# Ninety-six elementwise operations of a decoder layer's weight preparation put on GpSimd

## The chip, the cores and the metric

The kernel runs on one core of one Trainium2 chip. The metric is the device time of one execution in microseconds (us). The engines are TensorE (PE, with its weight loads as PEld), VectorE (DVE), ScalarE (ACT), GpSimd (POOL) and SyncE (SP), which issues nearly all DMA transfers.

## The reference

One decoder layer over 2048 tokens of width 1024, in float32:

```
h = rms_norm(x, mix_norm_g);  z = h @ w_in
y_lru = rg_lru(causal_dwconv(lru_x, 4 taps)) * gelu(lru_gate)
c     = silu(layer_norm(causal_dwconv(conf_a * sigmoid(conf_b), 31 taps)))
x = x + concat(y_lru, c) @ w_out

h = rms_norm(x, xa_norm_g);  m = rms_norm(mem, mem_norm_g)      # mem: 256 tokens
q = h @ w_q;  k, v = split(m @ w_kv)                            # 4 heads of 256
x = x + softmax(q k^T / 16) v @ w_o

h = rms_norm(x, ffn_norm_g);  g, u = split(h @ w_up)            # 2 x 3072
x = x + (gelu(causal_dwconv(g, 3 taps)) * u) @ w_down
return rms_norm(x, final_norm_g)
```

## The kernel before, in words

**Products.** Every large product is made of three matmuls on rounded operands: a value is split into a high part in TensorE's rounded format and a low part, the rest, and high by high, high by low and low by high are summed (`mm3`). `split(src, hi, lo)` does it: ScalarE copies the source into `hi`, VectorE subtracts `hi` from the source into `lo`. Tiles are 128 x 512.

**Tokens.** They are worked in four quarters of 512. A quarter's mixer computes the 31-tap convolution as 30 steps of VectorE on each of four blocks (`conf`), and the recurrence (`lru`). Quarters 0 and 1 then run `attend` alone. Quarters 2 and 3 run together in `attend_pair`, whose three products (with w_out, with the matrix A, with the matrix VO) are each done by seven block products in place of eight (`Folded`). Behind these come the up and down projections, more than half of the time, which use a like scheme.

**The matrices A and VO.** `memory_a` folds the query weights into the memory's keys, `memory_vo` the output weights w_o into its values. In `memory_vo`, for each of four heads, two pieces of w_o (128 x 1024, the tile `raw`) are loaded, each is split in two halves (tiles `wh`, `wl`), and TensorE multiplies the value rows (`kvh`, `kvl`) with them; the result is split again (`voh`, `vol`) and stored.

**The combined weights.** The seven products need sums and differences of blocks of the weights. `Folds.prepare` makes them once for each of the three matrices, as `F_out`, `F_a` and `F_vo`: for each of four block rows it gets four blocks by `block` (for w_out a load from memory, for A and VO the sum of the stored high and low parts, tile `wd`) and forms four sums or differences with `combine` (tiles `t`), which the SP queue stores as `t_out`, `t_a` and `t_vo`. `weight` fetches them back when the product comes and splits them. In each row T1 is the difference of two blocks, T3 and T2 need one block more (T2 needs T1 too), and T4 needs a fourth block and T2.

**The order of the work.** The kernel does not run its operations in the order of the program text. Tasks (generators) are stepped by a clock of TensorE's work; their operations are collected by `Program` and then planned: a list scheduler with a price for each operation and a due time worked back from TensorE's order gives each engine its fixed queue, and it also hands out the 84 buffers of 128 x 512. The order of the program text, and so the order in which buffers are handed out, depends on TensorE's clock alone. The prices for n columns are, in us, 0.15 + 0.0009 n for VectorE (0.2 for three-operand operations) and

```
    if eng == "Pool":
        return 0.18 + n * 0.0021
```

for GpSimd. No operation of the plan before is priced by this, since GpSimd gets none but some DMA issues at the start. All operations of the plan are emitted by one line, so the profile shows them as L399; they are told apart by their tiles.

Of the kernel before, what the change touches and what calls it, by code (L numbers as in the profile page):

```python
# [14 lines left out]
ALU = mybir.AluOpType  # L15
AX = mybir.AxisListType

P = 128
# [4 lines left out]
TT = 512  # L23
# [3 lines left out]
KH = D // P // 2  # L27
# [395 lines left out]
def hybrid_layer(  # L423
# [17 lines left out]
    pr = Program(nc, place)  # L441
# [4 lines left out]
    def V(name, *a, **k):  # L446
        pr.do("DVE", name, *a, **k)

    def ACT(out, in_, func, **k):
        pr.do("ACT", "activation", out, in_, func, **k)  # L450
# [14 lines left out]
    def ps():  # L465
        return pr.new("ps", name="ps")

    def tmp(name="tmp"):
        return pr.new("S", name=name)
# [4 lines left out]
    def pair(name, shape=None):  # L474
        return rnd(name + "h", shape), rnd(name + "l", shape)
# [99 lines left out]
        V("scalar_tensor_tensor", nsp[:], p[:], -2.0 * RG_C, neg[:], op0=ALU.mult, op1=ALU.add)  # L575


    def split(src, hi, lo):
        ACT(hi[:], src, AF.Copy)
        V("tensor_tensor", lo[:], src, hi[:].f32(), op=ALU.subtract)  # L580

    def split_scaled(src, g, hi, lo):
        ACT(hi, src, AF.Copy, scale=g)
# [2 lines left out]
    def mm3(p, wh, wl, xh, xl, start, stop, **k):  # L586
        matmul(p, wh, xh, start=start, stop=False, **k)
        matmul(p, wh, xl, start=False, stop=False, **k)
        matmul(p, wl, xh, start=False, stop=stop, **k)
# [44 lines left out]
    def raw_rows(w, r0):  # L634
        st = pr.new("W", (P, D), name="raw")
        pr.dma(st[:], w[r0 : r0 + P, :])
        return st

    def split_cols(st, f):
        hi, lo = pair("w", (P, KQ, P))  # L640
        split(st[:, :, f * P : (f + 1) * P], hi, lo)
        return hi, lo

    def flat(b):
# [2 lines left out]
    class Columns:  # L647
# [22 lines left out]
        def rounded(self, c0, kq, st):  # L670
            return [split_cols(st, f) for f in range(2)]
# [255 lines left out]
    def kv(c0):  # L927

        hi, lo = pair("kv")
        pp = [ps(), ps()]  # L930
        for kq in range(2):
            st = raw_cols(w_kv[0], c0, kq)
            for f in range(2):
                with together():
                    for k in range(KQ):
                        sl = slice((k % 2) * M, (k % 2 + 1) * M)
                        matmul(pp[f][:, :M], st[:, k, f * P : (f + 1) * P], mt[kq * 2 + k // 2][:, sl], start=kq + k == 0, stop=kq == 1 and k == KQ - 1)
            yield 0
        for f in range(2):
            fs = slice(f * M, (f + 1) * M)  # L940
            ACT(hi[:, fs], pp[f][:, :M], AF.Copy)
            V("tensor_tensor", lo[:, fs], pp[f][:, :M], hi[:, fs].f32(), op=ALU.subtract)
        return hi, lo

    def keep(rows, k, half, cols, src):

        base = (k * 2 + half) * 2
        for i in range(2):
            tok = rows.kept.tok.setdefault(base + i, Buf(None, (1,)))
            pr.dma(rows.kept.at(base + i)[:, cols], src[i].f32(), writes=[tok], join=True)  # L950
# [73 lines left out]
    def memory_vo():  # L1024
        yield mem_a
        yield VO_LATE
        for h in range(4):
            vh, vl = yield from kv(D + h * M)
            yield 1
            pp = [ps() for _ in range(4)]  # L1030
            for db in range(2):
                st = raw_rows(w_o[0], h * M + db * P)
                ww = []
                for half in range(2):
                    hi, lo = pair("w")
                    split(st[:, half * TT : (half + 1) * TT], hi, lo)
                    ww.append((hi, lo))
                for i, p in enumerate(pp):
                    mb, (wh, wl) = i // 2, ww[i % 2]
                    vs = slice(db * M + mb * P, db * M + (mb + 1) * P)  # L1040
                    with together():
                        mm3(p[:], vh[:, vs], vl[:, vs], wh[:], wl[:], db == 0, db == 1)
                    if i % 2:
                        yield 0
            for i, p in enumerate(pp):
                t = pair("vo")
                split(p[:], *t)
                keep(VO_rows, h * 2 + i // 2, i % 2, slice(0, TT), [b[:] for b in t])
# [276 lines left out]

    def combine(name, a, b, op):
        t = tmp(name)
        V("tensor_tensor", t[:], a, b, op=op)  # L1330
        return t

    UP_ORDER = ("B11", "B21", "T2", "T1", "T3", "T4", "B22")
# [237 lines left out]
    class Down:  # L1571
# [6 lines left out]
        def block(self, at, i):  # L1578
            m, f = at // NQ, at % NQ * KD + i
            t = tmp("h")  # L1580
            pr.dma(t[:], h_kept[f * P : (f + 1) * P, m * TT : (m + 1) * TT], reads=[h_tok[m // 2, f]])
            return t
# [71 lines left out]
    class Folds:  # L1654
# [5 lines left out]
        def block(self, k, half):  # L1660
            if self.rows.w is not None:
                t = tmp("wd")
                pr.dma(t[:], self.rows.w[k * P : (k + 1) * P, half * TT : (half + 1) * TT])
                return t
            hi, lo = self.rows.get(k, half)
            t = tmp("wd")
            V("tensor_tensor", t[:], hi[:].f32(), lo[:].f32(), op=ALU.add)
            return t

        def prepare(self, wait):  # L1670
            for i in range(KH):
                b11, b12 = self.block(i, 0), self.block(i, 1)
                t1 = combine("t", b12[:], b11[:], ALU.subtract)
                self.t.put(KH + i, t1[:])
                yield wait
                b22 = self.block(KH + i, 1)
                t3 = combine("t", b22[:], b12[:], ALU.subtract)
                t2 = combine("t", b22[:], t1[:], ALU.subtract)
                self.t.put(2 * KH + i, t3[:])
                self.t.put(i, t2[:])  # L1680
                yield wait
                t4 = combine("t", self.block(KH + i, 0)[:], t2[:], ALU.subtract)
                self.t.put(3 * KH + i, t4[:])
                del b11, b12, b22, t1, t2, t3, t4
                yield wait
            self.done.done = True
# [331 lines left out]
    m, n, a = mixers, normeds, attends  # L2018
# [6 lines left out]
    a[2].gen = attend_pair([n[2], attended[1]], [m[2], m[3], n[3]])  # L2025
    fold = Task(fold_weights())
    later.gen, mem_a.gen, mem_vo.gen = setup_later(), memory_a(), memory_vo()
    first_t.gen, first.gen, tail.gen = X[0].kept(a[1], T_PACE), first_x(), feed_forward()
    tasks.extend(TURNS())
# [33 lines left out]
```

## Time and profile before

| | us |
|---|---|
| median of 3 runs | 2397.0 (2396.76 to 2398.66) |
| span of the profiled execution | 2396.1 |
| granted TensorE clock, mean | 0.999 |
| busy: PEld | 1974.5 (82%) |
| busy: ACT | 1313.2 (55%) |

The profiled execution has no time of its own beside its span, which is 0.9 us under the median of the runs. A row of the profile names line, engine, operation and tiles (out<-in), the shapes, how often, and then busy time in us and the mean of one in ns; in a timeline it is start and length in us. A wait row names who waited, for whom, the total in us, how often and the longest. A matmul of 512 columns is recorded with 0.39 us, though the next one starts 0.23 us later: they overlap, and so do neighbouring VectorE operations, by less.

### The profile page before, as it was taken

To read this page: it belongs to the slowest core of one execution; us is meant where nothing else is said; L and a number is where in the kernel's file an instruction comes from. 1 tells how busy PE (TensorE), PEld (TensorE's weight loads), DVE (VectorE), ACT (ScalarE), POOL (GpSimd) and SP (SyncE) were. 2 spreads that over 40 slices of the span, in tenths; PEclk is the share of its full clock that TensorE was granted. 3 is DMA by queue.
4 is the path that set the end of the run, shared out by engine and by line. 5 is a ranking of instruction groups with operands and counts; after the bars stand their busy time and mean duration, and the time that the engine had idled before them with its cause. 6 is when DMAs were issued, how large, how long until landed. Compare 5 with 4: busy or idle time off the path is not lost.

```text
span 2396.1 us, 33483 instructions
## 1 busy us (share of the span) xinstructions
PE 2382.6 (99%) x10948; PEld 1974.5 (82%) x10948; DVE 2034.0 (85%) x3355; ACT 1313.2 (55%) x2374; POOL 11.2 (0%) x26
## 2 busy tenths in 40 slices
PE   9999999999999999999999999999999999999998
PEld 7898888888887888888888888888888888888887
DVE  7999994299899869879999887988988896676787
ACT  7772776357557678695555555554555541222333
POOL 1000000000000000000000000000000000000000
PEclk9999999999999999999999999999999999999999
DMA  9598789775878988787766544556565589887986
GB/s 351 197 296 309 234 300 305 254 255 176 296 261 271 318 277 280 268 289 265 252 234 208 194 172 158 175 177 211 190 216 199 186 303 324 283 280 254 312 303 258
DMA packets 363912, 604.56 MB, mean 252 GB/s; under 512 B 34809, under 2 KB 116985, under 8 KB 363738
## 3 DMA queue, kind: packets, MB, share of 16 engines
q1 hardware_dynamic: 362952, 601.81, 73.8%
q8 instruction: 86, 1.41, 0.2%
q14 instruction: 88, 0.72, 0.1%
q0 software_dynamic: 640, 0.36, 0.0%
q10 hardware_dynamic: 146, 0.27, 0.0%
HBM read 409.36 MB, written 192.94 MB: 251 GB/s over the span
## 4 chain that ended last, share of the span: by engine, by line
PE 94%; DVE 2%; ACT 2%; DMA 1%; issue 1%; SPq 0%; POOL 0%; DVEq 0%; POOLq 0%; ACTq 0%
PE ps L399 94%; DMA wl<-w_down 1%; DVE conv L399 1%; ACT L399 0%; DMA raw<-in_w_kv_dram 0%; ACT wh L399 0%; DVE wl L399 0%; ACT gate L399 0%; DVE x L399 0%; DVE s L399 0%; ACT yh L399 0%; DVE smalls L399 0%; DVE ptl L399 0%; ACT prob L399 0%; ACT conv L399 0%
## 5 line engine op out<-in xcount | busy, mean ns | idle before, releaser
L399 PE MATMUL ps<-Xh,wh 128*128 128x512 f32 x1344 | 523.3, 389 | 0.7 <-ACT u L399 0.7
L399 PE MATMUL ps<-Xh,wl 128*128 128x512 f32 x1344 | 523.2, 389 | 0.7 <-DVE wl L399 0.5
L399 PE MATMUL ps<-Xl,wh 128*128 128x512 f32 x1344 | 523.0, 389 | 0.0
L399 PE MATMUL ps<-wh,hidh 128*128 128x512 f32 x960 | 374.4, 390 | 0.0
L399 PE MATMUL ps<-wh,hidl 128*128 128x512 f32 x960 | 374.2, 390 | 0.1
L399 PE MATMUL ps<-wl,hidh 128*128 128x512 f32 x960 | 373.7, 389 | 0.0
L399 DVE SCALAR_TENSOR_TENSOR conv<-cb,v,conv 128x512 f32<-128x512 f32 x480 | 334.9, 741 | 1.8 <-ACT conv L399 0.9
L399 PEld LDWEIGHTS ps<-Xh,wl 128*128 128x128 f32 x1344 | 252.3, 188 | 54.0 <-DVE wl L399 1.5
L399 PEld LDWEIGHTS ps<-Xh,wh 128*128 128x128 f32 x1344 | 252.3, 188 | 53.1 <-ACT u L399 1.1
L399 PEld LDWEIGHTS ps<-Xl,wh 128*128 128x128 f32 x1344 | 252.3, 188 | 52.5
L399 ACT ACTIVATE hidh<-s 128x512 fp32r<-128x512 f32 x186 | 113.8, 631 | 271.6 <-DVE s L399 227.9
L399 PEld LDWEIGHTS ps<-wh,hidl 128*128 128x128 f32 x960 | 180.2, 188 | 39.5 <-DVE hidl L399 2.1
L399 PEld LDWEIGHTS ps<-wh,hidh 128*128 128x128 f32 x960 | 180.2, 188 | 37.8 <-ACT hidh L399 0.4
L399 PEld LDWEIGHTS ps<-wl,hidh 128*128 128x128 f32 x960 | 180.3, 188 | 37.2 <-DMA wl<-w_down 0.4
L399 PE MATMUL ps<-xh,wh 128*128 128x512 f32 x512 | 204.0, 398 | 0.1
L399 PE MATMUL ps<-xl,wh 128*128 128x512 f32 x512 | 199.6, 390 | 0.3 <-DVE xl L399 0.3
L399 PE MATMUL ps<-xh,wl 128*128 128x512 f32 x512 | 199.6, 390 | 0.0
L399 ACT ACTIVATE wh<-s 128x512 fp32r<-128x512 f32 x192 | 119.6, 629 | 117.6 <-DVE s L399 79.1
L399 ACT ACTIVATE wh<-raw 128x512 fp32r<-128x512 f32 (+2 forms) x214 | 127.4, 613 | 53.1 <-PE ps L399 21.6
L399 ACT ACTIVATE u<-ps 128x512 f32<-128x512 f32 x144 | 85.7, 595 | 126.0 <-PE ps L399 125.2
L399 DVE TENSOR_TENSOR acc<-acc,ps 128x512 f32<-128x512 f32 (+1 forms) x157 | 102.7, 678 | 59.5 <-PE ps L399 56.4
L399 DVE TENSOR_TENSOR wl<-raw,wh 128x512 fp32r<-128x512 f32 (+2 forms) x214 | 140.2, 668 | 12.0 <-ACT wh L399 10.7
(256 smaller groups left out, 4014.2 us busy)
## 6 DMA issues: line engine op xcount, KB each, us to landing
raw<-in_w_up_dram SPq DMA_DIRECT2D x96, 512.0 KB, 4.5
wh<-w_down SPq DMA_DIRECT2D x156, 256.0 KB, 4.9
wl<-w_down SPq DMA_DIRECT2D x156, 256.0 KB, 5.0
w_down<-wh SPq DMA_DIRECT2D x144, 256.0 KB, 3.1
w_down<-wl SPq DMA_DIRECT2D x144, 256.0 KB, 3.5
h<-hid SPq DMA_DIRECT2D x120, 256.0 KB, 4.7
wh<-w_in SPq DMA_DIRECT2D x96, 256.0 KB, 4.2
wl<-w_in SPq DMA_DIRECT2D x96, 256.0 KB, 4.7
```

The lines of the kernel that those rows point to most:

```text
L399: getattr(e, name)(*[resolve(a) for a in args], **{k: resolve(a) for k, a in kw.items()})
```

## The change

`split`, `split_cols` and `combine` get an argument for the engine that forms the difference, with VectorE as before where nothing is given. Three places give GpSimd: the low parts of w_o in `memory_vo`, the sum of high and low part in `Folds.block`, and the four sums and differences of `Folds.prepare`. `split_cols` takes the argument, and no caller gives one. ScalarE's half of a split stays. Since GpSimd's operations have other prices, the planner is run on other numbers and all queues can come out in another order.

```diff
-    def split(src, hi, lo):
+    def split(src, hi, lo, by="DVE"):
         ACT(hi[:], src, AF.Copy)
-        V("tensor_tensor", lo[:], src, hi[:].f32(), op=ALU.subtract)
+        pr.do(by, "tensor_tensor", lo[:], src, hi[:].f32(), op=ALU.subtract)
...
-    def split_cols(st, f):
+    def split_cols(st, f, by="DVE"):
         hi, lo = pair("w", (P, KQ, P))
-        split(st[:, :, f * P : (f + 1) * P], hi, lo)
+        split(st[:, :, f * P : (f + 1) * P], hi, lo, by)
         return hi, lo
...
                 for half in range(2):
                     hi, lo = pair("w")
-                    split(st[:, half * TT : (half + 1) * TT], hi, lo)
+                    split(st[:, half * TT : (half + 1) * TT], hi, lo, "Pool")
                     ww.append((hi, lo))
...
-    def combine(name, a, b, op):
+    def combine(name, a, b, op, by="DVE"):
         t = tmp(name)
-        V("tensor_tensor", t[:], a, b, op=op)
+        pr.do(by, "tensor_tensor", t[:], a, b, op=op)
         return t
...
             hi, lo = self.rows.get(k, half)
             t = tmp("wd")
-            V("tensor_tensor", t[:], hi[:].f32(), lo[:].f32(), op=ALU.add)
+            pr.do("Pool", "tensor_tensor", t[:], hi[:].f32(), lo[:].f32(), op=ALU.add)
             return t
...
         def prepare(self, wait):
             for i in range(KH):
                 b11, b12 = self.block(i, 0), self.block(i, 1)
-                t1 = combine("t", b12[:], b11[:], ALU.subtract)
+                t1 = combine("t", b12[:], b11[:], ALU.subtract, "Pool")
...
-                t3 = combine("t", b22[:], b12[:], ALU.subtract)
-                t2 = combine("t", b22[:], t1[:], ALU.subtract)
+                t3 = combine("t", b22[:], b12[:], ALU.subtract, "Pool")
+                t2 = combine("t", b22[:], t1[:], ALU.subtract, "Pool")
...
-                t4 = combine("t", self.block(KH + i, 0)[:], t2[:], ALU.subtract)
+                t4 = combine("t", self.block(KH + i, 0)[:], t2[:], ALU.subtract, "Pool")
```

## The prediction

> **What bounds the kernel now.** I read the page's first part, then the busy time by stretch in the places where the moved work runs, then what the weight loads of TensorE wait for there, then the single operations.
>
> ```profile
> span 2396.1 us, 33483 instructions
> ...
> PE 2382.6 (99%) x10948; PEld 1974.5 (82%) x10948; DVE 2034.0 (85%) x3355; ACT 1313.2 (55%) x2374; POOL 11.2 (0%) x26
> ...
> L399 DVE SCALAR_TENSOR_TENSOR conv<-cb,v,conv 128x512 f32<-128x512 f32 x480 | 334.9, 741 | 1.8 <-ACT conv L399 0.9
> ```
>
> TensorE is busy for 2382.6 of 2396.1 us, so all the time in which its records show it idle is 13.5 us. VectorE is at 85% on average and GpSimd idle; VectorE has the 480 steps of a 31-tap convolution, 0.74 us each, as its largest group. An average says little, so here are the four stretches that hold the moved work: the w_o halves (155 to 345 us), the sums for the first product (345 to 430), for the second (605 to 725) and for the third (725 to 970). Columns: stretch, length, then busy time and count for PE, PEld, DVE, ACT, POOL, clock, DMA share, GB/s.
>
> ```profile
> 155.00:345.00 190.00, 189.85 (x909) 158.27 (x908) 187.26 (x293) 112.64 (x201) 0.00 (x0) 1.00 0.83 281
> 345.00:430.00 85.00, 84.45 (x414) 70.85 (x414) 47.15 (x90) 45.78 (x111) 0.00 (x0) 1.00 0.90 305
> 605.00:725.00 120.00, 120.00 (x553) 98.49 (x552) 112.26 (x189) 65.62 (x124) 0.00 (x0) 1.00 0.85 285
> 725.00:970.00 245.00, 244.48 (x1169) 202.97 (x1168) 208.68 (x375) 188.88 (x401) 0.00 (x0) 1.00 0.84 289
> ```
>
> VectorE has 190 - 187.26 = 2.7 us free in the first stretch and 120 - 112.26 = 7.7 us in the third: it is full there. It has 37.9 us free in the second and 36.3 us in the fourth. TensorE is busy throughout in all four. So VectorE is the engine nearest to becoming a second bound, but TensorE sets the end, and taking work from VectorE pays only where TensorE waits for it. That is the next view: the waits ahead of the weight loads, first in the two early stretches, then in the two late ones (total us, times, longest).
>
> ```profile
> PEld ps L399 <- issue: 2.3, 7, 0.4
> PEld ps L399 <- DVE x L399: 0.8, 1, 0.8
> PEld ps L399 <- ACT gate L399: 0.6, 1, 0.6
> PEld ps L399 <- DVE xc L399: 0.4, 1, 0.4
> PEld ps L399 <- ACT xc L399: 0.4, 1, 0.4
> PEld ps L399 <- ACT yh L399: 0.4, 1, 0.4
> ```
>
> ```profile
> PEld ps L399 <- issue: 3.2, 10, 0.4
> PEld ps L399 <- DVE ptl L399: 0.6, 1, 0.6
> PEld ps L399 <- DVE sum L399: 0.5, 1, 0.5
> PEld ps L399 <- ACT prob L399: 0.5, 1, 0.5
> PEld ps L399 <- ACT xc L399: 0.4, 1, 0.4
> PEld ps L399 <- ACT gate L399: 0.4, 1, 0.4
> ```
>
> Waits that name VectorE: 0.8 + 0.4 + 0.6 + 0.5 = 2.3 us. Waits that name ScalarE: 0.6 + 0.4 + 0.4 + 0.5 + 0.4 + 0.4 = 2.7 us. Gaps in which nothing is named: 2.3 + 3.2 = 5.5 us, in seventeen pieces of at most 0.4 us. This is the whole of what the change can win in its own stretches: 10.5 us, of which 2.3 us hang on VectorE directly. A measurement of this kernel can tell some 0.2% from no change, which is 4.8 us.
>
> **The change, part by part.** What leaves VectorE can be counted by transfers: eight pieces of w_o, each split in two halves (16 low parts); three times 16 stored sums and differences (48); and 32 additions of a high and a low part, which the second and third products need and the first does not.
>
> ```profile
> L399 SPq DMA_DIRECT2D raw<-in_w_o_dram x8: 328/438/598, 159.6 to 288.3; - x8
> ...
> L399 SPq DMA_DIRECT2D t_out<-t x16: 319/382/473, 345.3 to 430.2; - x16
> ...
> L399 SPq DMA_DIRECT2D t_a<-t x16: 319/320/452, 611.0 to 720.4; - x16
> ...
> L399 SPq DMA_DIRECT2D t_vo<-t x16: 319/320/443, 729.6 to 965.0; - x16
> ...
> L399 DVE TENSOR_TENSOR wd<-wh,wl x32: 672/681/693, 609.0 to 963.3; 128x512 f32<-128x512 f32 x32
> ```
>
> That is 16 + 48 + 32 = 96 instructions of 128x512. One is recorded with 0.68 us. What it takes from the queue is less, since two in a row take 1.27 us:
>
> ```profile
> 247.70 1.15 ACT L399 ACTIVATE wh<-raw 128x512 fp32r<-128x512 f32 x2
> ```
>
> ```profile
> 251.11 1.27 DVE L399 TENSOR_TENSOR wl<-raw,wh 128x512 fp32r<-128x512 f32 x2
> ```
>
> ```profile
> 252.91 0.39 PE L399 MATMUL ps<-wl,kvh 128*128 128x512 f32 x1
> ```
>
> (The middle one of these three rows: less the 0.67 us of its second operation, 0.60 us from start to start.) So VectorE loses 96 x 0.60 = 57.6 us of work: 9.6 us in the first stretch, 9.6 in the second, 19.2 in the third and 19.2 in the fourth. Only the first and third parts, 28.8 us, lie where VectorE is full. Nothing of it shortens TensorE's own work; the number of matmuls stays. The freed time is not left empty: the planner gives a queue whatever is ready, and steps of the 31-tap convolution, which wait for no other engine, move up into it. So of the 2.3 us of waits on VectorE I count half as gone, 1.2 us: where such a wait goes, the ScalarE waits next to it in the two tables (a gate, an exponential, a rounded tile) are late next, and they stay.
>
> What GpSimd gains has no row of its own kind in the trace. The nearest are a fill of one column and a selection over 128 columns with one input:
>
> ```profile
> L2049 POOL MEMSET const-float32-1.0<- 128x1 f32 x1 | 0.1, 98 | 0.0
> ...
> masks.py:199 POOL TENSOR_SCALAR_AFFINE_SELECT ident<-ident 128x128 f32<-128x128 f32 x1 | 0.3, 323 | 0.1
> ```
>
> Fixed part 0.10 us, and (0.323 - 0.098) / 128 = 1.76 ns per column: 0.10 + 512 x 1.76 ns = 1.00 us for one input over 512 columns. If the second input costs another pass it is 1.90 us; if GpSimd were as quick as VectorE, 0.68 us. I take 1.25 us, an estimate nearer to the one-input row than to twice it because the row is the only one measured; it is also what the planner books for it (0.18 + 512 x 0.0021), so at this value the new order fits what it was planned for. GpSimd is then busy 96 x 1.25 = 120 us and is otherwise idle in these stretches, as the zeros of its column show. [...]
>
> Now the lateness. First the w_o halves. In the tightest of the four groups (the three rows above) ScalarE rounds both high parts by 247.70 + 1.15 = 248.85 us, VectorE comes to the low parts only at 251.11 and ends at 252.38, and TensorE first reads one at 252.91. GpSimd has no convolution ahead of them: two operations behind the roundings end by 248.85 + 2.50 = 251.35 us, and even at 1.90 us by 252.65. So this part costs nothing, by a margin of 0.3 us at the worst price.
>
> Second the sums. Each is stored by the SP queue and fetched back long after, for the first and the second product:
>
> ```profile
> L399 SPq DMA_DIRECT2D t_out<-t_out x16: 319/382/595, 794.8 to 850.9; - x16
> ...
> L399 SPq DMA_DIRECT2D t_a<-t_a x16: 319/320/424, 883.1 to 932.6; - x16
> ```
>
> The last stores stand at 430.2 and 720.4 us and the first fetches at 794.8 and 883.1 us, so 365 and 163 us cover them. The third has little: its last store is at 965.0 and its first fetch at 961.5. Fifteen of the operations that write or read a `wd` tile lie within 30 us (the third number is VectorE's busy time):
>
> ```profile
> 936.00:966.00 30.00, 10.14 (x15) 0.00 (x0) 1.00 0.95 341
> ```
>
> ```profile
> 965.55 0.32 SPq L399 DMA_DIRECT2D t_vo<-t_vo  x1
> ```
>
> ```profile
> L399 SPq DMA_DIRECT2D t_vo<-t_vo x16: 319/320/1021, 961.5 to 1006.5; - x16
> ...
> DMA to landing us min/median/max: 2.1/4.7/6.3
> ```
>
> ```profile
> 978.32 0.62 ACT L399 ACTIVATE wh<-t_vo 128x512 fp32r<-128x512 f32 x1
> ```
>
> Fifteen at 1.25 us are 18.8 us of GpSimd in those 30, so it keeps up. The longest row of dependent ones is five (two blocks, their difference, the next block, the difference of both), which come 5 x (1.25 - 0.60) = 3.3 us later. The fourth fetch for the product that follows is issued at 965.55, lands after a median of 4.7 us, at 970.3, and ScalarE rounds it at 978.32: 8.1 us of cover. It costs nothing at 1.25 us. The waits that the change adds stand in two queues. On GpSimd only its own later sums are queued behind them. On SP a store of a sum now waits for GpSimd, and behind it in that queue stand the fetches of the third product's weights; 3.3 us of delay stays inside the same cover.
>
> Last, the order of all engines is planned anew with other costs and is fixed before the run. That can close or open gaps such as the unnamed ones, 5.5 us either way; I take zero for it. The same for VectorE beside a reading GpSimd: the trace has no such pair. The bounds are nothing and the whole 1.25 us of each operation; I take nothing, because the row nearest to it, 672/681/693 ns for the additions while TensorE, ScalarE and the DMAs were busy beside them, shows no sign that neighbours stretch it.
>
> Sum: 2396.1 - 1.2 = 2394.9 us of span. The runs' median is 2397.0, 0.9 above the profiled span, so 2395.8, rounded 2396.0 us.
>
> **The rivals.** The first ends faster. Both named kinds of wait go, 5.0 us, with half of the unnamed gaps, 2.7 us, because what ScalarE works on comes through VectorE too and would move up: 2397.0 - 7.7 = 2389.3 us. For it: VectorE is full where the waits are. Against it: the waits that name ScalarE do not hang on the 96 themselves, and nearly all of the named waits must go before it can be told from no change.
>
> The second ends slower: VectorE is held while GpSimd reads. If each of the 96 stops VectorE for its whole time, VectorE gets 0.60 us back and loses 1.25: 0.65 us worse, 16 x 0.65 = 10.4 us in the first stretch and 32 x 0.65 = 20.8 us in the third. The free time there is 2.7 and 7.7 us, so VectorE comes 7.7 and 13.1 us late out of them. The chain that ended last runs through VectorE at just these ends:
>
> ```profile
> 353.30 0.61 DVE x L399
> ...
> 353.95 2.10 PE ps L399 x15
> ```
>
> ```profile
> 766.99 0.69 DVE sum L399
> ...
> 767.73 2.28 PE ps L399 x7
> ```
>
> TensorE takes up 0.04 and 0.05 us after VectorE's piece ends there, so what is late can reach it: up to 20.8 us, 2417.8 us. With half of it covered by matmuls that have their operands already (my choice between none and all), it is 2407.4 us. It decides from a hold of 0.60 + 2.7 / 16 = 0.77 us per operation on. Against it stands only that no row shows it. [...]
>
> The third also ends slower: an operation takes GpSimd 1.90 us. Then the fifteen need 28.5 of the 30 us, and at worst come 15 x (1.90 - 0.60) = 19.5 us late where 8.1 us are covered: 2397.0 + 11.4 = 2408.4 us. Against it: the planner would have to be wrong by half in its price.
>
> **How the numbers follow.** Forecast, no difference that can be told (2392.2 to 2401.8): 0.44. First rival: 0.20. Second: 0.28, high for a thing without a row, because its price is large and its place is where VectorE is full. Third: 0.08. So faster 0.20, same 0.44, slower 0.36. The range goes from 2391.0, which leaves out about half of the first rival, to 2416.0, which leaves out the full hold: about 0.18 in all. The likeliest case's own range is the 2392.2 to 2401.8 above.
>
> **What would show it.** Right: VectorE with 96 instructions fewer and 2034.0 - 96 x 0.68 = 1969 us; 96 operations on GpSimd near 1.25 us; durations of VectorE's operations unchanged at 0.68 and 0.74 us; the same TensorE busy time. First rival: the lists of waits ahead of weight loads empty in 155 to 430 and 605 to 970 us. Second: VectorE's mean for the convolution steps well above 0.74 us and TensorE waiting for VectorE near 350, 725 and 767 us. Third: GpSimd busy 180 us and the weight loads waiting near 970 us. The forecast is wrong if the time lies outside 2392.2 to 2401.8.

## The result, and the profile after

The changed kernel takes 2441.1 us (median of 5 runs, 2436.32 to 2442.38). The kernel before, run beside it, takes 2397.0 us (5 runs, 2396.59 to 2398.66). The ratio is 1.0178, with a 95% interval of 1.0166 to 1.0191: the change makes the kernel 44 us slower. The forecast was no difference that can be told, 2396.0 us, and the range ended at 2416.0: both were wrong.

The page of the changed kernel, the lines that answer to those of before: the span, the busy time by engine, the group of the convolution steps (busy us, mean ns of one, idle before).

```profile
span 2436.5 us, 33602 instructions
...
PE 2396.8 (98%) x10948; PEld 1980.4 (81%) x10948; DVE 2030.7 (83%) x3259; ACT 1312.9 (54%) x2374; POOL 180.8 (7%) x122
...
L399 DVE SCALAR_TENSOR_TENSOR conv<-cb,v,conv 128x512 f32<-128x512 f32 x480 | 366.5, 810 | 1.3
```

The counts are as forecast: VectorE has 96 instructions fewer (3355 to 3259), GpSimd 96 more, TensorE the same 10948 matmuls. The times are not. VectorE lost 96 instructions of 0.68 us in its records and is busy 2030.7 us where 2034.0 - 65 = 1969 us were expected, because others became longer: the 480 convolution steps alone by 366.5 - 334.9 = 31.6 us. The reader should note that VectorE's total, taken by itself (2034.0 and 2030.7 us), looks as if nothing had happened to it.

The busy time in the same four stretches (stretch, length, then PE, PEld, DVE, ACT, POOL with counts, clock, DMA share, GB/s):

```profile
155.00:345.00 190.00, 183.22 (x851) 151.15 (x850) 185.08 (x273) 107.82 (x191) 21.53 (x12) 0.97 0.77 260
345.00:430.00 85.00, 81.36 (x384) 67.61 (x383) 45.54 (x69) 44.39 (x105) 23.87 (x17) 0.98 0.86 296
605.00:725.00 120.00, 113.35 (x521) 92.84 (x520) 110.55 (x158) 54.41 (x110) 58.61 (x25) 0.97 0.68 234
725.00:970.00 245.00, 235.68 (x1093) 192.35 (x1092) 192.12 (x305) 180.93 (x342) 43.23 (x26) 0.99 0.82 278
```

TensorE, which was idle for 1.2 us in these four stretches before, is now idle for 6.8 + 3.6 + 6.7 + 9.3 = 26.4 us, and its granted clock is no longer 1.00 in any of them. In the third stretch VectorE does 158 instructions in 110.55 us where it did 189 in 112.26: 0.70 us each where it was 0.59.

What the weight loads of TensorE wait for, in 155 to 430 us and then in 605 to 970 us (total us, times, longest):

```profile
PEld ps L399 <- DVE x L399: 4.7, 4, 3.3
PEld ps L399 <- DVE xl L399: 4.6, 3, 3.2
PEld ps L399 <- ACT xh L399: 3.5, 1, 3.5
PEld ps L399 <- issue: 2.6, 8, 0.4
```

```profile
PEld ps L399 <- ACT prob L399: 8.9, 4, 4.8
PEld ps L399 <- DVE xl L399: 6.0, 4, 3.0
...
PEld ps L399 <- ACT xh L399: 2.8, 2, 1.9
PEld ps L399 <- DVE ptl L399: 2.2, 2, 1.7
```

The named waits, which came in pieces of at most 0.8 us before, have become waits of up to 4.8 us, for tiles that VectorE makes (`x`, `xl`) or that ScalarE makes from what VectorE made late (`xh`, `prob`). None names GpSimd. The unnamed gaps are nearly as before (2.6 and 3.4 us in the two windows, 2.3 and 3.2 before).

Long waits have a second cost. This is TensorE's timeline around one of them (start us, length us):

```profile
264.11 0.39 PE L399 MATMUL ps<-wh,kvl 128*128 128x512 f32 x1
267.61 0.49 PE L399 MATMUL ps<-xh,gwh 64*128 64x512 f32 x2 [3.12 <-ACT xh L399]
...
272.02 0.63 PE L399 MATMUL ps<-xl,wh 128*128 128x512 f32 x1
272.44 0.63 PE L399 MATMUL ps<-xh,wl 128*128 128x512 f32 x1
...
275.31 0.39 PE L399 MATMUL ps<-xh,wh 128*128 128x512 f32 x1
275.53 0.39 PE L399 MATMUL ps<-xl,wh 128*128 128x512 f32 x1
```

And the busy time of that stretch, in which the granted clock (third number from the end) is 0.50:

```profile
268.40:275.10 6.70, 6.18 (x16) 4.39 (x17) 6.70 (x12) 4.57 (x8) 0.00 (x0) 0.50 0.88 288
```

After 3.12 us without a matmul the next ones start 0.42 us apart, where 0.22 us is usual, until 275.3 us. There are five such stretches in the trace, from 176.2 (3.4 us), 268.3 (6.8), 367.3 (3.4), 695.0 (6.8) and 735.9 us (3.4): 23.9 us at half clock with the lengths unrounded, so 11.9 us of matmul time lost. The waits of TensorE just ahead of them are 2.84, 3.12, 3.08, 4.39 and 2.70 us long. The kernel before has no such stretch ahead of its last microseconds. The mean clocks say about the same, as far as their three digits go: 2436.5 x (1 - 0.994) = 14.6 us after against 2396.1 x (1 - 0.999) = 2.4 us before. What makes the clock fall the records do not show, and the length of the one wait ahead does not settle it: in this trace a wait of 1.65 us that ended at 762.33 us had no such stretch behind it (granted clock 1.00 from 757 to 773 us), and in e8, an experiment below, the clock fell after two waits of 0.68 and 0.63 us (start us, length us; in the last two rows the matmuls are 0.43 us apart):

```profile
669.08 0.47 PE L404 MATMUL ps<-wh,xah 128*128 128x512 f32 x1 [0.68 <-DMA wh<-A]
...
670.93 0.71 PE L404 MATMUL ps<-wh,xah 128*128 128x512 f32 x1 [0.63 <-DMA wh<-A]
...
672.59 0.63 PE L404 MATMUL ps<-wh,xah 128*128 128x512 f32 x1
673.02 0.63 PE L404 MATMUL ps<-wl,xah 128*128 128x512 f32 x1
```

So the span's 40.4 us are about 25 us in which TensorE waits (26.4 - 1.2 in the four stretches) and 12 us of half clock; about 3 us lie outside them or were not assigned. TensorE's busy time says so too: it grew by 2396.8 - 2382.6 = 14.2 us for the same matmuls.

**What stretches VectorE.** Timelines of VectorE and of GpSimd over the same few microseconds, in the third stretch:

```profile
654.63 7.84 DVE L399 SCALAR_TENSOR_TENSOR conv<-cb,v,conv 128x512 f32<-128x512 f32 x7
```

```profile
656.41 1.45 POOL L399 TENSOR_TENSOR wd<-wh,wl 128x512 f32<-128x512 f32 x1 [7.17 <-DMA wl<-A]
657.93 1.62 POOL L399 TENSOR_TENSOR t<-wd 128x512 f32<-128x512 f32 x1
659.51 1.74 POOL L399 TENSOR_TENSOR t<-wd,t 128x512 f32<-128x512 f32 x1
```

Seven convolution steps that follow each other take 6 x 0.66 + 0.74 = 4.70 us when nothing disturbs them (23 such steps elsewhere in this trace take 15.32 us, 0.66 each). Here they take 7.84: 3.14 us lost beside three GpSimd operations, 1.05 us each. GpSimd pays too: the three take 1.45 to 1.74 us, where the same operation beside an idle VectorE takes 1.29:

```profile
439.06 1.29 POOL L399 TENSOR_TENSOR t<-wd,t 128x512 f32<-128x512 f32 x1 [2.33 <-DMA wd<-in_w_out_dram]
```

A convolution step reads two tiles in SBUF. Where VectorE reads PSUM and one SBUF tile, nothing is lost: three operations take 2.07 us, 0.69 each, beside two GpSimd operations that take their usual 1.3. In all, 49 VectorE operations that read PSUM ran beside GpSimd's sums in this trace (for at least 30% of their length), and none is longer than the median of its group before by more than 0.03 us.

```profile
629.53 2.07 DVE L399 SCALAR_TENSOR_TENSOR xal<-ps,v,xah 128x512 fp32r<-128x512 f32 x3 [1.18 <-ACT xah L399]
```

```profile
629.12 1.30 POOL L399 TENSOR_TENSOR wd<-wh,wl 128x512 f32<-128x512 f32 x1 [4.93 <-DMA t_a<-t]
630.49 1.28 POOL L399 TENSOR_TENSOR t<-wd 128x512 f32<-128x512 f32 x1
```

Small operations on statistics are held as well, though they have one input: 317 ns each on average where it was 174. Their group before, and then after:

```profile
L399 DVE TENSOR_SCALAR smalls<-smalls 128x2 f32<-128x2 f32 (+2 forms) x55 | 9.1, 174 | 0.8 <-ACT smalls L399 0.3 <-ACT junk L399 0.2
```

```profile
L399 DVE TENSOR_SCALAR smalls<-smalls 128x2 f32<-128x2 f32 (+2 forms) x55 | 16.9, 317 | 1.0 <-ACT smalls L399 0.3 <-ACT junk L399 0.2
```

Each VectorE instruction of the trace was set against the median of its group before (same operation, tiles and shape): 59 are longer by more than 0.05 us, by 51.1 us together. This sum is called the stretch below. 32.3 us of it are in convolution steps and 7.7 us in these small operations; the longest of the small ones took 1.31 us.

### The profile page after: what moved, and what is told of

Same layout as the page of the kernel before. It is cut to its first block, busy times and chain, and to the rows that moved or that the text cites. A ratio compares the mean times of both kernels' runs of the same rounds, so it can differ in the third digit from the quotient of the medians.

```text
span 2436.5 us, 33602 instructions
## 1 busy us (share of the span) xinstructions
PE 2396.8 (98%) x10948; PEld 1980.4 (81%) x10948; DVE 2030.7 (83%) x3259; ACT 1312.9 (54%) x2374; POOL 180.8 (7%) x122
## 4 chain that ended last, share of the span: by engine, by line
PE 83%; DVE 10%; ACT 3%; DMA 2%; issue 1%; SPq 0%; DVEq 0%; ACTq 0%
PE ps L399 83%; DVE conv L399 5%; DMA wl<-w_down 1%; DVE s L399 1%; ACT prob L399 1%; DVE smalls L399 1%; DVE gate L399 1%; ACT gate L399 0%; DVE xc L399 0%; DVE wl L399 0%; DVE hidl L399 0%; DMA h<-hid 0%; ACT L399 0%; DVE al L399 0%; DVE cv L399 0%
## 5 line engine op out<-in xcount | busy, mean ns | idle before, releaser
L399 DVE SCALAR_TENSOR_TENSOR conv<-cb,v,conv 128x512 f32<-128x512 f32 x480 | 366.5, 810 | 1.3
L399 ACT ACTIVATE wh<-raw 128x512 fp32r<-128x512 f32 (+2 forms) x214 | 127.2, 613 | 55.0 <-PE ps L399 18.3
L399 DVE TENSOR_TENSOR wl<-s,wh 128x512 fp32r<-128x512 f32 x192 | 130.2, 688 | 21.9 <-ACT wh L399 18.1
```

The source lines that it names most:

```text
L399: getattr(e, name)(*[resolve(a) for a in args], **{k: resolve(a) for k, a in kw.items()})
```

## The experiments

The theory from the profile: VectorE is held while GpSimd reads, and as the planner knew nothing of that, it had already filled the freed 57.6 us with other work. The rivals: the new order is bad in itself; GpSimd's results come too late; the freed VectorE time is what matters. The change and all sixteen experiments, with the stretch and the time at half clock ahead of the last microseconds, in us (both summed from each kernel's trace):

| run | what it is | us | ratio (95%) | stretch | half clock |
|---|---|---|---|---|---|
| | the change | 2441.1 | 1.0178 (1.0166 to 1.0191) | 51.1 | 23.9 |
| e1 | new order, additions on VectorE | 2424.4 | 1.0114 (1.0098 to 1.0131) | 0 | 20.5 |
| e2 | old order, additions on GpSimd | 2415.9 | 1.0081 (1.0066 to 1.0096) | 56.1 | 13.7 |
| e3 | GpSimd only writes | 2398.0 | 1.0004 (0.9994 to 1.0013) | 0.3 | 0 |
| e4 | before, and GpSimd does all again | 2448.2 | 1.0215 (1.0199 to 1.0230) | 62.7 | 30.7 |
| p1 | w_o halves alone | 2409.4 | 1.0052 (1.0037 to 1.0067) | 12.9 | 10.2 |
| p2 | first product's sums alone | 2404.3 | 1.0034 (1.0021 to 1.0047) | 5.5 | 6.8 |
| p3 | second product's alone | 2419.6 | 1.0094 (1.0079 to 1.0109) | 18.3 | 13.7 |
| p4 | third product's alone | 2402.0 | 1.0022 (1.0013 to 1.0032) | 12.3 | 0 |
| e5 | booked at 1.1 us, planned anew | 2414.6 | 1.0071 (1.0056 to 1.0086) | 52.7 | 13.7 |
| e6 | GpSimd reads one input | 2406.2 | 1.0040 (1.0027 to 1.0053) | 15.2 | 0 |
| e7 | GpSimd writes three times | 2397.5 | 0.9999 (0.9989 to 1.0008) | 2.0 | 0 |
| e8 | p3 with fills, two of them long | 2401.3 | 1.0021 (1.0011 to 1.0030) | 0.9 | 3.4 |
| e9 | p3 planned anew, VectorE waits for each result | 2429.1 | 1.0133 (1.0118 to 1.0149) | 21.7 | 27.3 |
| e10 | before, and GpSimd reads, nobody waits for it | 2469.1 | 1.0299 (1.0284 to 1.0315) | 49.8 | 47.8 |
| e11 | e10 without the reading | 2427.7 | 1.0129 (1.0112 to 1.0146) | 0 | 17.1 |
| e12 | p3's order, additions on VectorE | 2412.1 | 1.0063 (1.0048 to 1.0078) | 0 | 10.2 |

The kernel before took 2396.9 to 2397.7 us in these runs.

Whether two kernels have the same order can be read from their traces, from the names of the tiles of VectorE's operations in turn (without the statistics and without tiles of the names that the 96 write). e1, e3, e6 and e7 have the order of the change, e2 that of before, and e8 and e12 that of p3, in all 2763 places. The change differs from before in 350 places and e4 in 130. e5 differs from e2 in 543, e9 from p3 in 2169 and e11 from before in 1983: these are other orders as well, and their times hold what the order does. e10 and e11 differ from each other in 15.

**The order and the hold apart.** e1 keeps every queue as the change has it and only issues the 96 operations on VectorE, at the places that the plan gave them on GpSimd:

```diff
-                e = self.engines[o.on]
+                e = self.engines["DVE" if o.on == "Pool" and o.calls[0][0] == "tensor_tensor" else o.on]
```

> The order of every queue is that of the changed kernel, but the 96 operations stand in VectorE's queue at their planned places, so GpSimd reads nothing beside VectorE. Theory of the hold (VectorE and GpSimd shut each other out while both read SBUF, VectorE falls behind where it is full, TensorE waits and then runs at half clock): 2397 to 2410 us, VectorE's convolution step back at 0.74 us. Theory of the order (the newly planned order is the worse one): about 2441 us. Theory of lateness (GpSimd's results come too late): 2395 to 2400 us.

The group of the convolution steps in e1:

```profile
L399 DVE SCALAR_TENSOR_TENSOR conv<-cb,v,conv 128x512 f32<-128x512 f32 x480 | 335.5, 743 | 1.2
```

No step is longer, and yet the kernel is 27.5 us slower than before, more than expected. VectorE has 57.6 us of work that the order did not allow for, and that alone costs half as much.

e2 does the opposite: planned as VectorE's, in the old order, and issued on GpSimd.

```diff
-            o = self.op("Pool" if eng == "either" else eng)
+            o = self.op("Pool" if eng == "either" else "DVE" if eng == "moved" else eng)
+            o.moved = eng == "moved"
...
-                e = self.engines[o.on]
+                e = self.engines["Pool" if o.moved else o.on]
```

> Every queue is planned as before, with the 96 operations priced and placed as VectorE's, and they are then put on GpSimd at those places. Hold: slower than before by 30 us or more, 2427 to 2450 us, convolution steps of 1.7 us beside GpSimd's operations. Order: about 2397 us. Lateness: 2410 us or more, but with VectorE's steps at 0.74 us.

Its convolution steps:

```profile
L400 DVE SCALAR_TENSOR_TENSOR conv<-cb,v,conv 128x512 f32<-128x512 f32 x480 | 369.4, 815 | 2.4 <-ACT conv L400 0.9
```

The steps are stretched as in the change, but 2415.9 us is less than the 2427 us or more that was expected. VectorE gets 57.6 us back and loses 56.1, so that its total stays, and the kernel is still 19 us slower: what is given back at one place does not pay for what is lost at another, where VectorE was full.

**GpSimd that writes and does not read.** e3 takes the changed kernel and puts a fill in the place of each of the 96 (the differences and sums are left out).

```diff
+                    if o.on == "Pool" and name == "tensor_tensor":
+                        e.memset(resolve(args[0]).bitcast(F32), 0.0)
+                        continue
```

> The changed kernel with each of the 96 operations replaced by a GpSimd fill of the same output, which reads nothing; the 96 sums and differences are left out. Hold: 2390 to 2400 us, VectorE's steps at 0.74 us. Order: about 2441 us. Lateness: 2390 to 2400 us as well, since a fill is short and early, so this run does not part those two.

Two groups of e3, the convolution steps and one of the three groups of fills:

```profile
L402 DVE SCALAR_TENSOR_TENSOR conv<-cb,v,conv 128x512 f32<-128x512 f32 x480 | 333.7, 741 | 1.3
...
L400 POOL MEMSET t<- 128x512 f32 x48 | 24.6, 527 | 83.5 <-PE ps L402 72.6 <-DMA t_a<-t 6.3 <-DMA VO<-voh 3.0
```

This run says three things. The new order is not bad in itself. The reading is what stretches VectorE's convolution steps (741 ns each on average here as before, 810 in the change). And with the 96 gone from VectorE, nothing late and next to nothing held, the time is that of before: the most that this change could have won in the order planned for it is nothing that can be told. No other order of all 96 was run with fills.

A fill takes 0.53 us, so that its results come earlier than those of an addition. e7 therefore fills each tile three times, 1.6 us:

```diff
+                        for _ in range(3):
+                            e.memset(resolve(args[0]).bitcast(F32), 0.0)
```

> The changed kernel with each of the 96 operations replaced by three GpSimd fills of the same output, 3 x 0.53 = 1.6 us, which read nothing; the sums and differences are left out. GpSimd is as long at each as in the changed kernel. Hold: 2395 to 2400 us. Lateness: 2430 us or more, as each result comes as late as there.

2397.5 us: that results come as late as those of an addition (1.29 us) costs nothing. The fills hold something too, which was not expected: nine small operations on statistics are longer, by up to 0.42 us and 2.0 us together, and nothing else is. Their group in e7:

```profile
L403 DVE TENSOR_SCALAR smalls<-smalls 128x2 f32<-128x2 f32 (+2 forms) x55 | 10.6, 214 | 1.0 <-ACT smalls L403 0.3 <-ACT junk L403 0.2
```

e6 lets GpSimd read, but one input (a copy of the first; the second is left out):

```diff
+                    if o.on == "Pool" and name == "tensor_tensor":
+                        name, args, kw = "tensor_copy", args[:2], {}
```

> The changed kernel with each of the 96 operations replaced by a GpSimd copy of its first input; the second input is left out of the sums. Hold, if reading is what counts: GpSimd's copies stretch VectorE's steps as the sums do, by their own length of 0.6 to 1.0 us; 2410 to 2435 us. Hold, if it takes two inputs on GpSimd: about 2397 us. Lateness: between the two, with VectorE's steps at 0.74 us.

The copies by tile (ns, least, median, most):

```profile
L401 POOL COPY t<-wd x48: 616/620/1202, 338.3 to 957.5; 128x512 f32<-128x512 f32 x48
...
L401 POOL COPY wd<-wh x32: 612/640/10883, 602.5 to 955.8; 128x512 f32<-128x512 f32 x32
```

One input holds VectorE too, for less: 15.2 us of stretch and +9 us, from an operation half as long (0.62 us against 1.29). That is less than the 2410 us or more that was expected. The copies are shut out in their turn, one of them for 10.9 us (the last number of the second row).

**More of it.** e4 is the kernel before, in which GpSimd does each of the 96 operations once more into a tile that nobody reads. VectorE is not relieved.

```diff
+    def again(a, b, op):
+        pr.do("Pool", "tensor_tensor", spare[:], a, b, op=op)
```

> The kernel before, with the 96 operations on VectorE as they were, and each done a second time on GpSimd into a tile that nobody reads. Hold: as slow as the changed kernel or slower, 2440 to 2480 us, since VectorE saves nothing and loses about 1 us for each. Order: near 2397 us, as the order is nearly that of before. Lateness: near 2397 us, as no one waits for the results.

51 us slower: the hold without any relief of VectorE costs somewhat more than the change. What the relief pays back depends on the order. e2, which has the relief in the order of before, costs 19.0 us, some 32 less than e4 in nearly that order; in the change's own order, which has other work in the freed time, the loss is 44.1. In e4 the input tiles are also kept longer by GpSimd, so e10 has it read a tile of its own. ScalarE writes a mark when a result is there, GpSimd clears the mark and adds a tile of zeros to itself, and nobody waits for it.

```diff
+        m = small(1)
+        pr.first = True
+        ACT(m[:], done[:, :1], AF.Copy)
+        pr.first = False
+        pr.do("Pool", "memset", m[:], 0.0)
+        pr.do("Pool", "tensor_tensor", spare[:], spare[:], spare[:], op=ALU.add, reads=[m])
```

> The kernel before with all its work on VectorE; behind each of the 96 operations ScalarE copies one column into a mark, GpSimd clears the mark and then adds a tile of zeros to itself. Nobody waits for GpSimd and it keeps no buffer. If the stretching of VectorE's steps counts: 2425 to 2450 us, near the 2448.2 us of the run in which the 96 were done twice. If late GpSimd operations count: 2397 to 2402 us.

```profile
L399 POOL TENSOR_TENSOR spare<-spare 128x512 f32<-128x512 f32 x96 | 126.0, 1312 | 1.8
```

2469.1 us, more than expected, but the marks cost something too. e11 is e10 without the last line:

> The control for the hold alone: the same 96 marks by ScalarE and their clearing by GpSimd, without GpSimd's additions. If the additions cost by stretching VectorE's steps: 2397 to 2415 us, the marks being small, against 2469.1 us with the additions. If the marks themselves cost (ScalarE waits in its queue for VectorE at each): 2440 us or more.

The 96 marks, their clearing and the order that was planned with them cost 30.5 us, far more than expected; e11 has another order than before, and what the marks cost by themselves is not told apart from it. e10 has nearly the order of e11. The reading itself is the difference between the two, 2469.1 - 2427.7 = 41.4 us, for 49.8 us of stretch. As a price of the hold in the kernel before this is sound only if it is the same in that other order, which no run shows; e4's 51 us for 62.7 us of stretch is near the same share (0.82 and 0.83), with VectorE's own work unrelieved in both.

**Booking the hold.** e5 is e2 with each of the 96 planned as if VectorE were busy for 1.1 us, which gives it an order of its own:

```diff
+            if eng == "moved":
+                o.cost = 1.1
```

> The 96 operations are planned as VectorE's at 1.1 us each, about what a hold takes from VectorE, and then put on GpSimd at those places: the plan expects the loss. Hold: 2400 to 2412 us, less than the 2415.9 us of the old order that did not expect it, as VectorE no longer falls behind its plan. Order: any order goes, about 2397 us. Lateness: as the old order, about 2416 us.

2414.6 us (2411.7 to 2416.8) against 2415.9: hardly better, which was not expected. The stretch is there all the same (52.7 us). Why a booked hold does not help stays open; that the booked time stands at the addition's own place in VectorE's queue, and the hold falls on whatever VectorE does when GpSimd gets to run, is an argument and was not tried, and neither was e5's order without the hold.

**The four parts alone.** Each moves one of the four groups and leaves the others on VectorE.

```diff
+            self.by = "Pool" if name in ("t_a",) else "DVE"
...
-            pr.do("Pool", "tensor_tensor", t[:], hi[:].f32(), lo[:].f32(), op=ALU.add)
+            pr.do(self.by, "tensor_tensor", t[:], hi[:].f32(), lo[:].f32(), op=ALU.add)
```

(here the second product's; `t_out` and `t_vo` for the first and the third, and the argument in `memory_vo` alone for w_o.)

> Only the 16 low parts of w_o are put on GpSimd, the rest stays on VectorE; the order is planned for that. Hold, with TensorE losing about half a microsecond for each that VectorE has beyond its plan: 16 holds of about 1 us in a full stretch, 2402 to 2408 us. Rival, that the loss sits only where the second product's softmax meets VectorE: 2397 us.

> Only the 16 sums and differences for the first product are put on GpSimd, most of them where VectorE is half empty. Hold: 2396 to 2401 us, since only the first few fall where VectorE is full. Rival of the second product's place: 2397 us.

> Only the 32 operations for the second product are put on GpSimd, where VectorE is full. Hold: 32 holds of about 1 us, 2409 to 2418 us. Rival of the second product's place: nearly the whole loss, 2430 us or more.

> Only the 32 operations for the third product are put on GpSimd; about a quarter of them fall where VectorE is full, the others later. Hold: 2398 to 2407 us. Rival of the second product's place: 2397 us.

12.4 + 7.4 + 22.7 + 5.1 = 47.6 us, against the change's 44.1: the parts nearly add up, and all four cost, also the first and the third product's, where VectorE had over 36 us free. Three of the four came out above the range that was expected of the hold, p1 by 1.4 us, p2 by 3.3 and p3 by 1.6. Nearly half of the loss is the second product's, and not nearly all of it, as the rival there had it. Its trace shows the reverse of the hold. VectorE and GpSimd over the same time:

```profile
635.77 27.25 DVE L399 SCALAR_TENSOR_TENSOR conv<-cb,v,conv 128x512 f32<-128x512 f32 x41
662.94 0.69 DVE L399 TENSOR_REDUCE smalls<-ps 128x2 f32<-128x512 f32 x1
```

```profile
639.86 24.31 POOL L399 TENSOR_TENSOR wd<-wh,wl 128x512 f32<-128x512 f32 x1 [7.83 <-DVE conv L399]
664.25 1.62 POOL L399 TENSOR_TENSOR t<-wd 128x512 f32<-128x512 f32 x1
```

Forty-one convolution steps run at 0.66 us without a sign of disturbance, and an addition that GpSimd could start at 639.86 us, beside the last 35 of them, ends 24.3 us later, when VectorE has turned to a tile in PSUM (662.94 us; the addition ends 1.23 us later, about the length of one undisturbed). In the change the longest is 12.2 us. What waits behind it is the SP queue, which has the store of the sum and then the loads of other weights. SP's waits and the chain from 639 to 674 us, both of p3:

```profile
SPq L399 <- POOL wd L399: 26.7, 6, 19.2
...
SPq L399 <- POOL t L399: 18.8, 6, 14.4
```

```profile
639.89 24.28 POOL wd L399
...
664.25 1.62 POOL t L399
...
665.89 0.32 SPq L399
...
666.26 2.77 DMA wl<-w_in
...
669.08 3.93 PE ps L399 x10
```

So a weight load of another product, `wl<-w_in`, is issued late, and TensorE takes it up 0.05 us after it lands. How much of p3's 22.7 us is this? e8 has p3's order with fills in place of the sums (which are left out), 3 for each, but 46 (24 us) for the twelfth and 23 (12 us) for the twenty-third: GpSimd late by the two long operations of p3, with no reading.

```diff
+            fills = iter([3] * 11 + [46] + [3] * 10 + [23] + [3] * 9)
...
+                    if o.on == "Pool" and name == "tensor_tensor":
+                        for _ in range(next(fills)):
+                            e.memset(resolve(args[0]).bitcast(F32), 0.0)
+                        continue
```

> The kernel with the second product's 32 operations alone on GpSimd, in its order, but each replaced by GpSimd fills of its output that read nothing: 3 fills for most (1.6 us), 46 (24.3 us) for the twelfth and 23 (12.1 us) for the twenty-third, the times that these two took there behind VectorE's convolution steps. The 32 sums and differences are left out. If such a late GpSimd operation holds up the SP queue and with it the weights: 2405 to 2416 us, TensorE waiting for DMAs near 670 and 710 us. If only the stretching of VectorE's steps counts: about 2397 us.

SP's wait for the fills in e8:

```profile
SPq L404 <- POOL t L402: 24.7, 3, 16.8
```

The longest wait, 16.8 us, is near p3's two (19.2 and 14.4), the sum is about half of p3's 45.5 us. So much lateness costs 4.4 us of the 22.7, 1.7 of them by the half clock shown above, and the time lies between the two that were expected; p3's own lateness, with more waits, may cost more. e12 is p3's order with the sums issued on VectorE, by the line of e1:

> The order planned for the second product's 32 operations on GpSimd, with these in VectorE's queue at their planned places: no hold, no late GpSimd, but 32 x 0.60 = 19.2 us of VectorE's time that the plan did not expect. If time that VectorE loses against its plan is the main channel: 2408 to 2416 us. If it is the late operations of GpSimd: 2397 to 2402 us.

14.8 us for 32 x 0.60 = 19.2 us of VectorE's time that the order does not allow for, as expected; in p3 the hold takes 18.3 us in its place. If the two add up, which no run shows, e12's 14.8 and e8's 4.4 us make 19.2 of the 22.7. The rest, 3.5 us, may be the lateness that e8 does not have, or that a hold strikes at other places than an addition; it is not told apart.

e9 keeps GpSimd from being shut out: in p3, VectorE copies one column of each result at once, and so has to wait for GpSimd there.

```diff
+    def meet(by, t):
+        if by == "Pool":
+            pr.first = True
+            V("tensor_copy", mark[:], t[:, :1])
+            pr.first = False
+        return t
```

> The second product's 32 operations on GpSimd, and VectorE made to copy one column of each result at once, so that it waits for GpSimd and cannot pass it with convolution steps for 12 or 24 us. If the loss goes through late GpSimd operations: 2400 to 2412 us, none of them over 4 us. If it goes through VectorE's lost time: 2420 us or more, as VectorE loses up to 1.3 us for each of 32.

The longest GpSimd operation falls to 6.6 us (none over 4 was expected, if lateness was the channel), and the kernel gets slower still, 2429.1 us. That fits the view that to let GpSimd through costs more than its lateness, since it is VectorE's time that TensorE waits for. It does not show it: the copies made the planner find quite another order (2169 of 2763 places), and no run has that order without them.

## Why the prediction was wrong, step by step

**The step that failed** is the last one ahead of the sum: "The same for VectorE beside a reading GpSimd ... I take nothing". The bounds there were nothing and 1.25 us of each operation, and the row that chose between them was that of VectorE's additions beside TensorE, ScalarE and the DMAs. None of these is GpSimd, so the row could not speak to the question. Measured: 1.05 us lost for each of the three GpSimd operations at 656 us, and 51.1 us over the whole kernel, 0.53 for each of the 96 on average. With fills in place of the sums, in the same order, the 44 us are gone (e3, e7).

**The second rival**, given 0.28, had the mechanism, and its price was too low: 2407.4 to 2417.8 us, against 2441.1. Its hold was not too small: it took 1.25 us for each operation, and by its own sum the measured 0.53 would be less than the 0.60 us that VectorE gets back and would cost nothing. What failed is this setting of gain against loss. The gain was already spent: the prediction itself says that the planner fills the freed time with convolution steps, and this was not carried into the rival. e1 shows what VectorE time that the order does not allow for is worth: 27.5 us for 57.6. The rival also charged only the first and third stretches, where VectorE's average leaves nothing free; the other two cost 7.4 and 5.1 us (p2, p4). A free 36 us in a stretch do not help the tile that TensorE is waiting for at that moment. And it had no half clock, which is 12 us here: the waits of 2.7 to 4.4 us ahead of it are dearer than their length.

**Right, or free as forecast.** The 96 operations leave VectorE, and the gain from this is nothing that can be told (e3: 1.0004, 0.9994 to 1.0013; the forecast had 1.2 us). One operation takes GpSimd 1.29 us alone (1.25 forecast), and as late as that its results harm nobody (e7). The new order by itself is worth zero (e3, e7). The list of waits was a bound from above for what could be won, and a high one: by TensorE's records only 1.2 us of the four stretches were idle, so most of the 10.5 us of waits lay under matmuls that ran, and the 7.7 us of the first rival were hardly there to win. What the prediction missed is that the list says nothing about what could be lost.

**The first rival** falls: the waits did not go, and e3 shows that in this order a VectorE that is free of the 96 gains nothing that can be told. **The third** falls as it was put (1.90 us for each, and the third product late): GpSimd is busy 180.8 us as that rival's sign says, but because it is shut out for some operations (two of 12.2 and 11.7 us, with a median of 1.45), not because each takes 1.90 us. The place was another one too, the second product's stores on SP, and what of it was tried cost 4.4 us (e8). The step on SP's queue, "3.3 us of delay stays inside the same cover", holds for 3.3 us and not for 24.

**What stays open.** The change's 44 us are not fully taken apart. e1 (27.5 us, no hold) and e2 (19 us, old order) make 46.5 together, but each has its own order or its own load, and that they add up may be chance. What is shown is that with the 96 on GpSimd the change's order is 25.2 us slower than that of before (2441.1 against e2's 2415.9), though the stretch is smaller (51.1 against 56.1 us) and though the same order costs nothing where no one is held (e3). The stretch of 51.1 us costs 44 us, and e1's 57.6 us of unplanned additions only 27.5: that holds strike where VectorE is tightest would fit, and was not tested by itself. The 12 us of half clock are read from rows; no run held the clock and kept the waits. And why GpSimd gets through between convolution steps at one place (656 us) and is shut out for some 35 of them at another was not tried.

## What to carry to other kernels

Before work is moved to an idle engine, replace it there by something that hardly holds its neighbours (here a fill: 0.3 us of stretch in e3, 2.0 in e7): that run shows about the most that the move can win in the order it has, and if this is nothing a cost need not be priced to know that the move does not pay in that order. An idle engine is not a free one: ask which reads and writes of its neighbours it will meet, and give the unseen pair a price from both ends rather than from a row with other neighbours. In an order fixed ahead of the run, freed time is spent by the planner at once, so a cost that the planner does not know has nothing to be set against: 57.6 us of it cost 27.5 us here (e1), and 19.2 us cost 14.8 (e12). To book it is not a sure way out (e5). And look at the clock after each wait of TensorE: waits of 2.7 to 4.4 us were paid again in clock here, and in e8 two of less than 0.7 us.

## What the runs showed of the hardware

- VectorE's convolution steps, which read two SBUF tiles, and GpSimd's sums, which read SBUF, lengthened each other: 1.05 us lost to VectorE for each of three GpSimd operations, which took 1.45 to 1.74 us themselves and take 1.29 us alone. GpSimd fills did not lengthen such steps (the 480 are busy for 334.9 us before, 333.7 in e3, 334.2 in e7 and 366.5 in the change), and VectorE operations that read PSUM were not lengthened by GpSimd's sums (49 in the change, none longer by more than 0.03 us).
- GpSimd can be held far longer than that, and the runs show no bound: one GpSimd addition took 24.3 us in p3 beside some 35 convolution steps that ran at their usual 0.66 us.
- VectorE's TENSOR_SCALAR operations on statistics (55, most of them 128x2) went from a mean of 174 to 317 ns, the longest to 1.31 us, about the 1.29 us of one GpSimd addition. Fills lengthened these too: 214 ns on average in e7.
- GpSimd, 128x512 in f32, undisturbed: addition of two tiles 1.29 us, copy 0.62 us, fill 0.53 us.
- TensorE fell to half clock (granted 0.50) after waits of 2.70 to 4.39 us in the change, and in e8 after two of 0.68 and 0.63 us. After a wait of 1.65 us in the change it did not fall. It stayed at half for 3.4 us (three times) or 6.8 us (twice) in the change, and in e9 for 27.3 us in all.
